# Attention tiles split into queries with keys and values, and loaded behind the score products of the step before

## The chip, the cores and the metric

One core of a Trainium2 chip runs the kernel; the seven others are idle. The metric is the device time of one execution in microseconds (us). The kernel before took 2695.2 us (median of 3 runs, 2694.12 to 2695.24).

## The reference

One layer of a hybrid decoder block on 2048 tokens of width 1024, all in float32. The change touches branch A, the attention:

```
h = RMSNorm_pre(x) * (1 + scale) + shift
q|k|v, mLSTM q|k|v|o, i|f, g_A, g_B = split(h W_in)
branch A: 8 query heads of 64 on 2 key/value heads, rotary on q and k,
          causal window of 128 in blocks of 128:
  s = q . [k of the block before | k of this block] / 8, masked
  m = max(max(s), sink);  p = exp(s - m);  p = p / (sum(p) + exp(sink - m))
  y_A = p . [v of the block before | v of this block]
branch B: conv4 + SiLU, chunkwise mLSTM, head norm, output gate -> y_B
x = x + gate * RMSNorm_post((sigmoid(g_A) y_A W_A + sigmoid(g_B) y_B W_B) W_out)
x = x + gate * RMSNorm_post(SwiGLU FFN of the normed x)
```

A block of 128 queries is one attention tile n, so there are 16 of them.

## The kernel before, in words

Every large product is written as three products of split operands (a high and a low part), so that TensorE is the engine with the most work. The first half of the program (up to about 1400 us) works on two superblocks of 1024 tokens, each of two blocks of 512 tokens. Per block it projects h with slices of `w_in`: keys and values with the gates (`tx` of 264 columns), attention queries, the mLSTM values (`vm`), and so on. The weights arrive in `raw` and are split on ScalarE and VectorE into `whi` and `wlo` (L263 to L267); the products add up in PSUM tiles `acc`, of which there are four, and ScalarE copies each out to a `tx` (L798 for keys, values and gates, L773 for queries, L819 for the mLSTM values). The rotated q, k and v of tile n are written to a DRAM buffer `at_d[n]`, by SyncE's queue (SP): 1024 columns of q (high and low part), 512 of k (high and low), 256 of v.

Attention is then a generator per stream. Stream 0 takes the even tiles and stream 1 the odd ones. One tile goes through these steps (lines of before; `attention` at L887):

- SP loads all of it, 128 x 1792, into one tile `at` (L900; the first tile of all in three pieces, L895 and L898), and the stream asks for `L_LOAD` = 5000 ns before the next step.
- TensorE makes the scores, 24 products from `at` into four PSUM tiles `mix` (L211); ScalarE copies the half that needs no mask (L923), VectorE masks the other half (L925) and takes the maximum (L930 to L933).
- ScalarE takes exp, one activation per head (L938), VectorE the sums and reciprocals (L940, L941), GpSimd normalises in two halves of four heads (L942). The stream asks for `L_SOFT` = 8000 ns.
- TensorE transposes each half (L216, `mix<-ident,tm`); ScalarE and VectorE split it (L951, L955).
- TensorE multiplies with v, which is read from the same `at` (L211, `mix<-tm,at`); L964 and L965 split the result, and SP stores it (L967).

`at` has two buffers, one per stream in effect. So the load of tile n+2 waits until the last product with v of tile n has read its `at`, and it is issued only then.

The order is decided in two stages. `run2` (L351) walks through the large products in small groups; after each group, `tick` (L230) goes on with those streams whose due time has come on a modelled clock. `finish` (L237) and `end_attention` run streams to their end with no large product between. A scheduler then puts the instructions of each engine in order. In what follows S, T and V with a number stand for the score products, the transposes and the products with v of that tile. Tiles 8 to 15 belong to superblock 1; tiles 8 to 11 run beside the projections of its second block.

Of the kernel before, what the change touches and what calls it, by code (L numbers as in the profile page):

```python
# [10 lines left out]
F32 = mybir.dt.float32  # L11
F32R = mybir.dt.float32r
# [7 lines left out]
P = 128  # L20
# [4 lines left out]
NT = TB // P  # L25
# [19 lines left out]
L_LOAD, L_HP2, L_HC = 5000.0, 1000.0, 3000.0  # L45
# [27 lines left out]
def decoder_block(ctx: ExitStack, tc: tile.TileContext, a: dict, out: bass.AP, dbg=None):  # L73
    nc = tc.nc
# [38 lines left out]
    def nm(s):  # L113
        uid[0] += 1
        return f"{s}{uid[0]}"
# [576 lines left out]
    def at():  # L692
        return kvp.tile([P, AT_N], F32R, tag="at", name=nm("at"), bufs=2)
# [34 lines left out]
    def superblock(sb):  # L728
# [158 lines left out]
        def attention(n):  # L887
            first = n == 0
# [3 lines left out]
            a_ = at()  # L892
            af = a_.bitcast(F32)
            if first:
                nc.sync.dma_start(af[:, :AT_K], at_d[n][:, :AT_K])  # L895
                for c0, k in ((AT_K, 2), (AT_V, 1)):
                    v_, d_ = (z[:, c0:c0 + 2 * k * P].rearrange("p (i u k) -> p i u k", i=k, u=2)[:, :, 1, :] for z in (af, at_d[n]))
                    nc.sync.dma_start(v_, d_)  # L898
            else:
                nc.sync.dma_start(af, at_d[n])  # L900
            qth, qtl = (a_[:, i * 512:(i + 1) * 512].rearrange("p (j q) -> p j q", j=GQ) for i in range(2))
            kth, ktl = (a_[:, AT_K + 2 * i * P:AT_K + 2 * (i + 1) * P] for i in range(2))
            vat = af[:, AT_V:].rearrange("p (u d) -> p u d", u=2)
            yield L_LOAD
# [6 lines left out]
            for jj in range(2):  # L911
# [14 lines left out]
                if jj == 0:  # L926
                    yield 0
            for g in range(2):
                hs = slice(g * GQ, (g + 1) * GQ)
                V.tensor_reduce(mx[:, hs], sc[g], axis=AX.X, op=ALU.max)  # L930
# [28 lines left out]
            for src_, u, st_, sp_ in ((pfs, int(first), True, first), (pcs, 1, False, True)):  # L959
                for g, p_ in enumerate(src_):  # L960
                    mm(yps[g * 64:(g + 1) * 64, :], vat[:, u, g * 64:(g + 1) * 64], p_.rearrange("p j q -> p (j q)"), st_, sp_)
            now[0] -= 1500.0
# [3 lines left out]
            for i, y in enumerate((yh, yl)):  # L966
                nc.sync.dma_start(y_d[b][:, i, :, t * P:(t + 1) * P], y.bitcast(F32).rearrange("p (j q) -> p j q", j=GQ))  # L967

        ready = [0]

        def attention_stream(u):
            for i in range(u, 2 * NT, 2):
                while i >= ready[0]:
                    yield 1000.0
                yield from attention(b0 * NT + i)
                done_att[0] += 1
                yield 500.0
# [1121 lines left out]
```

## Time and profile before

| what | value |
|---|---|
| median of 3 runs | 2695.2 us |
| the profiled execution | 2696.74 us |
| its span on the core | 2695.0 us |
| mean granted TensorE clock | 0.992 |
| TensorE (PE) busy | 2635.9 us, 98% |
| VectorE (DVE) busy | 1986.3 us, 74% |
| ScalarE (ACT) busy | 1297.2 us, 48% |
| GpSimd (POOL) busy | 136.8 us, 5% |
| moved by DMA | 511.89 MB, mean 190 GB/s |

The profiled execution lies 1.74 us above its span (what lies around the first and the last instruction) and 1.5 us above the median. A row of the timeline gives start, duration, engine, line, operation, `out<-in`, partitions x elements and a count of equal instructions in a row; behind it, in square brackets, stands how long the engine was idle before the row, and which instruction ended that idle time. A row of the waits gives the total, the number and the longest. In a table of windows there stands, for each engine, its busy time in that stretch, then the granted TensorE clock as a share of full speed.

### The profile page before, as it was taken

The page shows a single profiled execution, that of the slowest core. Times are in us where ns is not written, and L with a number is a line of the kernel's source. Part 1 is how long each engine was busy: PE and PEld are TensorE (multiplying, and loading weights), DVE is VectorE, ACT ScalarE, POOL GpSimd, SP SyncE. Part 2 cuts the span into 40 slices and gives each one's busy share as a digit, 9 for nine tenths or more (in the row PEclk, how much of TensorE's full clock was granted, in tenths as well). Part 3 has the DMA queues.
Part 4 walks back from the last instruction along what each step waited for, and adds up shares of the span by engine and source line. Part 5 has one row for each costly group of instructions (what it writes and reads, how often), then busy time and mean ns, then how long its engine had stood idle before and what let it go on. Part 6 is the DMA issues. An engine that isn't in the chain of part 4 may idle for free.

```text
span 2695.0 us, 35854 instructions
## 1 busy us (share of the span) xinstructions
PE 2635.9 (98%) x12382; PEld 2149.4 (80%) x12382; DVE 1986.3 (74%) x3882; ACT 1297.2 (48%) x2525; POOL 136.8 (5%) x181
## 2 busy tenths in 40 slices
PE   7899999999998999999999999999999999999998
PEld 6777788888885778888887888887877888888886
DVE  7888887768686888876687777776677676766466
ACT  4657544545754554444563443334554333333444
POOL 0100001100101000110000000000000000000000
PEclk9999999999998999999999999999999999999999
DMA  7574456897574644677775564436675232324566
GB/s 251 172 236 138 147 176 185 267 341 243 188 246 145 204 139 139 204 250 284 243 233 192 178 201 160 153 118 215 213 272 187 98 118 88 111 98 145 191 207 219
DMA packets 353637, 511.89 MB, mean 190 GB/s; under 512 B 25120, under 2 KB 213660, under 8 KB 348208
## 3 DMA queue, kind: packets, MB, share of 16 engines
q1 hardware_dynamic: 353288, 509.55, 57.2%
q8 instruction: 97, 1.59, 0.2%
q14 instruction: 84, 0.69, 0.1%
q10 hardware_dynamic: 168, 0.06, 0.0%
HBM read 357.12 MB, written 144.02 MB: 186 GB/s over the span
## 4 chain that ended last, share of the span: by engine, by line
PE 84%; DVE 6%; DMA 4%; ACT 2%; issue 1%; POOL 0%; SPq 0%; DVEq 0%; POOLq 0%; ACTq 0%
PE acc L211 59%; PE mix L211 22%; PE mix L216 2%; DVE hl L1589 1%; DMA at_d<-tx 1%; DMA raw<-as_d 1%; DMA tx<-in_w_ada_dram 1%; ACT hl L1588 1%; DMA at<-at_d 1%; DMA raw<-in_w_ffn_down_dram 1%; DVE wlo L267 0%; DMA raw<-ws_d 0%; DMA big<-big 0%; DVE tm L925 0%; DVE big L1589 0%
## 5 line engine op out<-in xcount | busy, mean ns | idle before, releaser
L211 PE MATMUL acc<-big,hl 128*128 128x512 f32 x3936 | 939.5, 393 | 2.3 <-ACT hl L1588 0.9
L211 PEld LDWEIGHTS acc<-big,hl 128*128 128x128 f32 x3936 | 732.8, 188 | 168.5 <-issue 9.0
L1588 ACT CAST hl<-raw 128x512 fp32r<-128x512 f32 x732 | 440.2, 621 | 494.9 <-PE acc L211 227.9
L1589 DVE TENSOR_TENSOR hl<-raw,hl 128x512 fp32r<-128x512 f32 x732 | 497.9, 696 | 196.5 <-ACT hl L1588 194.1
L211 PE MATMUL acc<-whi,big 128*128 128x512 f32 (+1 forms) x1216 | 356.2, 374 | 7.7 <-ACT tx L89 3.8
L211 PE MATMUL mix<-big,hl 128*128 128x512 f32 x1056 | 262.9, 390 | 1.7 <-ACT hl L1588 1.0
L211 PEld LDWEIGHTS acc<-whi,big 128*128 128x128 f32 x1216 | 222.0, 190 | 49.7 <-ACT tx L89 4.3
L211 PE MATMUL acc<-hl,hl 128*128 128x512 f32 x1008 | 237.3, 393 | 5.9 <-DVE hl L1589 3.3
L211 PEld LDWEIGHTS mix<-big,hl 128*128 128x128 f32 x1056 | 197.8, 188 | 44.4 <-ACT hl L1588 1.9
L211 PE MATMUL acc<-wlo,big 128*128 128x512 f32 (+1 forms) x608 | 225.9, 374 | 3.5 <-DVE wlo L267 3.5
L211 PEld LDWEIGHTS acc<-hl,hl 128*128 128x128 f32 x1008 | 187.0, 188 | 51.6 <-DVE hl L1589 8.7
L211 PE MATMUL mix<-hl,hl 128*128 128x512 f32 x792 | 182.3, 390 | 1.2 <-DVE ms L455 0.5
L211 PEld LDWEIGHTS mix<-hl,hl 128*128 128x128 f32 x792 | 148.0, 188 | 34.5 <-DVE hl L1589 2.9
L211 PE MATMUL acc<-big,whi 128*128 128x512 f32 x512 | 157.3, 393 | 0.0
L267 DVE TENSOR_TENSOR wlo<-raw,whi 128x1024 fp32r<-128x1024 f32 (+1 forms) x95 | 108.8, 1146 | 60.4 <-ACT whi L266 54.7
L266 ACT CAST whi<-raw 128x1024 fp32r<-128x1024 f32 (+1 forms) x95 | 93.7, 987 | 116.0 <-PE acc L211 104.7
L211 PEld LDWEIGHTS acc<-wlo,big 128*128 128x128 f32 x608 | 115.6, 190 | 24.1 <-DVE wlo L267 5.0
L457 POOL TENSOR_TENSOR rs<-ms,halves 128x1 f32<-128x1 f32 (+1 forms) x56 | 42.9, 779 | 1657.0 <-DVE ms L455 1647.2
L211 PE MATMUL mix<-hcT4h,hl 128*128 128x512 f32 x352 | 115.6, 389 | 0.7 <-ACT hl L1588 0.7
L211 PE MATMUL acc<-hcT2h,hl 128*128 128x512 f32 x352 | 115.5, 389 | 0.0
L211 PEld LDWEIGHTS acc<-big,whi 128*128 128x128 f32 x512 | 95.3, 188 | 19.2
L211 PE MATMUL acc<-big,wlo 128*128 128x512 f32 x256 | 97.5, 392 | 0.0
(350 smaller groups left out, 3544.2 us busy)
## 6 DMA issues: line engine op xcount, KB each, us to landing
raw<-in_w_in_dram SPq DMA_DIRECT2D x48, 1024.0 KB, 5.6
as_d<-w SPq DMA_DIRECT2D x154, 256.0 KB, 2.0
raw<-as_d SPq DMA_DIRECT2D x70, 512.0 KB, 3.9
raw<-in_w_ffn_gate_dram SPq DMA_DIRECT2D x22, 1024.0 KB, 5.7
raw<-in_w_ffn_up_dram SPq DMA_DIRECT2D x22, 1024.0 KB, 5.5
raw<-ws_d SPq DMA_DIRECT2D x40, 512.0 KB, 4.6
y_d<-tm SPq DMA_DIRECT2D x64, 256.0 KB, 3.7
tx<-in_w_ada_dram SPq DMA_DIRECT2D x64, 256.0 KB, 4.2
```

Source lines behind the costliest of these rows:

```text
L211: T.matmul(o, lhsT=lhsT, rhs=rhs, start=start, stop=stop, skip_group_check=resumed)
L216: T.transpose(o, i, ident[:k, :k])
L266: A.copy(hv, src)
L267: V.tensor_tensor(lv, src, hv.bitcast(F32), op=ALU.subtract)
L457: G.tensor_tensor(r[:, :n], ms[:, :n], nhalf[:, :n], op=ALU.pow)
L1588: A.copy(v(hi), src)
L1589: V.tensor_tensor(v(lo), src, v(hi).bitcast(F32), op=ALU.subtract)
```

## The change

`at` is split into two tiles: `at` (q and k, 128 x 1536) and `av` (v, 128 x 256), with two buffers each and the same space in all. The score products read `at`, the products with v read `av`; so the buffer of q and k comes free with the scores of its tile. Where the stream's next tile n+2 lies in a block that is ready (n = 0, 1, 4, 5 within a superblock of eight tiles), `load_qk(n + 2)` is issued right behind the score products of n, and `load_v(n + 2)` behind its products with v; the stream then goes to the next tile without `L_LOAD`. These loaded-ahead tiles are n = 2, 3, 6, 7 and 10, 11, 14, 15. The eight others (0, 1, 4, 5, 8, 9, 12, 13) are loaded when the stream begins or finds its block ready, in two DMAs instead of one, with `L_LOAD` behind them. Nothing else is edited; lines behind L889 move by up to 23 (scores' copy L936, exp L953, normalising L957, keys' copy L801, queries' copy L776, mLSTM values' copy L822). Every engine has the same instructions in both programs, but SP, which issues 15 DMAs more.

```diff
--- before.py
+++ after.py
@@ -689,8 +689,11 @@
 
     AT_K, AT_V, AT_N = 2 * 512, 2 * 512 + 4 * P, 2 * 512 + 6 * P
 
-    def at():
-        return kvp.tile([P, AT_N], F32R, tag="at", name=nm("at"), bufs=2)
+    def at_qk():
+        return kvp.tile([P, AT_V], F32R, tag="at", name=nm("at"), bufs=2)
+
+    def at_v():
+        return kvp.tile([P, AT_N - AT_V], F32, tag="av", name=nm("av"), bufs=2)
 
     def ld(shape, dtype=F32):
         t = kvp.tile([P, 512], dtype, tag="ld", name=nm("ld"), bufs=4)
@@ -884,24 +887,34 @@
             R["gates", b] = negm_d, mp, cl, ex
 
 
-        def attention(n):
+        def load_qk(n):
+            a_ = at_qk()
+            af = a_.bitcast(F32)
+            if n == 0:
+                nc.sync.dma_start(af[:, :AT_K], at_d[n][:, :AT_K])
+                v_, d_ = (z[:, AT_K:AT_V].rearrange("p (i u k) -> p i u k", i=2, u=2)[:, :, 1, :] for z in (af, at_d[n]))
+                nc.sync.dma_start(v_, d_)
+            else:
+                nc.sync.dma_start(af, at_d[n][:, :AT_V])
+            return a_
+
+        def load_v(n):
+            v_ = at_v()
+            if n == 0:
+                nc.sync.dma_start(v_[:, P:], at_d[n][:, AT_V + P:])
+            else:
+                nc.sync.dma_start(v_, at_d[n][:, AT_V:])
+            return v_
+
+        def attention(n, a_, av, ahead):
             first = n == 0
             b, t = divmod(n, NT)
             k0 = P if first else 0
             ks = slice(k0, 2 * P)
-            a_ = at()
-            af = a_.bitcast(F32)
-            if first:
-                nc.sync.dma_start(af[:, :AT_K], at_d[n][:, :AT_K])
-                for c0, k in ((AT_K, 2), (AT_V, 1)):
-                    v_, d_ = (z[:, c0:c0 + 2 * k * P].rearrange("p (i u k) -> p i u k", i=k, u=2)[:, :, 1, :] for z in (af, at_d[n]))
-                    nc.sync.dma_start(v_, d_)
-            else:
-                nc.sync.dma_start(af, at_d[n])
+            later = None
             qth, qtl = (a_[:, i * 512:(i + 1) * 512].rearrange("p (j q) -> p j q", j=GQ) for i in range(2))
             kth, ktl = (a_[:, AT_K + 2 * i * P:AT_K + 2 * (i + 1) * P] for i in range(2))
-            vat = af[:, AT_V:].rearrange("p (u d) -> p u d", u=2)
-            yield L_LOAD
+            vat = av.rearrange("p (u d) -> p u d", u=2)
             mx = small.tile([P, HQ], F32, tag="mx", name=nm("mx"))
             nm_ = small.tile([P, HQ], F32, tag="nmx", name=nm("nmx"))
             sums = small.tile([P, HQ], F32, tag="sums", name=nm("sums"))
@@ -925,6 +938,8 @@
                     V.copy_predicated(dst, mk, negc.unsqueeze(1).to_broadcast([P, 2, P]) if first else bv[:, :, :P])
                 if jj == 0:
                     yield 0
+            if ahead():
+                later = load_qk(n + 2)
             for g in range(2):
                 hs = slice(g * GQ, (g + 1) * GQ)
                 V.tensor_reduce(mx[:, hs], sc[g], axis=AX.X, op=ALU.max)
@@ -959,20 +974,28 @@
             for src_, u, st_, sp_ in ((pfs, int(first), True, first), (pcs, 1, False, True)):
                 for g, p_ in enumerate(src_):
                     mm(yps[g * 64:(g + 1) * 64, :], vat[:, u, g * 64:(g + 1) * 64], p_.rearrange("p j q -> p (j q)"), st_, sp_)
+            if later is not None:
+                later = later, load_v(n + 2)
             now[0] -= 1500.0
             yh, yl = tm([P, 512], F32R), tm([P, 512], F32R)
             A.copy(yh, yps)
             V.tensor_tensor(yl, yps, yh.bitcast(F32), op=ALU.subtract)
             for i, y in enumerate((yh, yl)):
                 nc.sync.dma_start(y_d[b][:, i, :, t * P:(t + 1) * P], y.bitcast(F32).rearrange("p (j q) -> p j q", j=GQ))
+            return later
 
         ready = [0]
 
         def attention_stream(u):
+            tiles = None
             for i in range(u, 2 * NT, 2):
-                while i >= ready[0]:
-                    yield 1000.0
-                yield from attention(b0 * NT + i)
+                n = b0 * NT + i
+                if tiles is None:
+                    while i >= ready[0]:
+                        yield 1000.0
+                    tiles = load_qk(n), load_v(n)
+                    yield L_LOAD
+                tiles = yield from attention(n, *tiles, lambda: i + 2 < ready[0])
                 done_att[0] += 1
                 yield 500.0
 
```

On TensorE the two programs differ in two stretches, one in each superblock (in time about 95 to 290 us and 775 to 990 us); all that stands between and behind them has the same order. Three places follow.

**TensorE, tiles 10 and 11.** In these rows `at_7797` is tile 10 and `at_7831` tile 11, `tm_7840` and `tm_7841` are the two halves of the probabilities of tile 10, `tm_7918` and `tm_7919` those of tile 11. Before, from the last score product of tile 11 to the first of its products with v:

```order
L211 MATMUL mix_7939<-at_7831 128x256
L216 MATMUL mix_7997<-ident,tm_7840 128x128 x4
L216 MATMUL mix_8027<-ident,tm_7841 128x128 x4
L211 MATMUL mix_8042<-tm_8002,at_7797 64x512
L211 MATMUL mix_8042<-tm_8032,at_7797 64x512
L211 MATMUL mix_8042<-tm_8004,at_7797 64x512
L211 MATMUL mix_8042<-tm_8034,at_7797 64x512
L216 MATMUL mix_8053<-ident,tm_7918 128x128 x4
L216 MATMUL mix_8071<-ident,tm_7919 128x128 x4
L211 MATMUL mix_8089<-tm_8058,at_7831 64x512
```

After, the rows from the last scores of tile 11 on; `at_7724` is its q and k, `tm_7826` and `tm_7827` belong to tile 10, and `acc_8288` is one of the four tiles of the query projection:

```order
L211 MATMUL acc_8288<-whi_8379,big_7150 128x512
L211 MATMUL mix_7937<-at_7724 128x256 x6
L216 MATMUL mix_7980<-ident,tm_7826 128x128 x4
L216 MATMUL mix_7999<-ident,tm_7827 128x128 x4
L211 MATMUL acc_8288<-wlo_8380,big_7150 128x512
L211 MATMUL acc_8288<-whi_8379,big_7151 128x512
```

Before, S10, S11, T10, V10, T11 and V11 stood in one block, with no large product between them from S10 to the first `acc` behind V11. After, products of the query projection and of `vm` stand between nearly all of them (17 between T10 and V10, 6 between V10 and T11), and the loads of q and k of tiles 10 and 11 stand on SP behind S8 and S9.

**ScalarE, between the keys and the queries of superblock 1's second block.** `acc_8016` to `acc_8019` are the four PSUM tiles of the key and value projection, `tm_7587` and `tm_7588` the scores of tile 8. Before:

```order
L263 CAST whi_8170<-raw_7745 128x2x4x64 x2
L798 COPY tx_8182<-acc_8016 128x264
L881 ACT_TABLE_LOAD
L881 ACTIVATE ex_7654<-ex_7654 128x48
L798 COPY tx_8204<-acc_8017 128x264
L798 COPY tx_8224<-acc_8018 128x264
L263 CAST whi_8257<-raw_7745 128x2x4x64 x2
L798 COPY tx_8244<-acc_8019 128x264
L938 ACTIVATE tm_7587,sums_7585<-tm_7587,nmx_7584 128x128
L934 ACTIVATE es_7586<-es_7586 128x8
L938 ACTIVATE tm_7587,sums_7585<-tm_7587,nmx_7584 128x128 x3
L938 ACTIVATE tm_7588,sums_7585<-tm_7588,nmx_7584 128x128 x4
```

After, where the four are `acc_8088` to `acc_8091`, the scores of tile 8 are `tm_7606` and `tm_7607`, and those of tile 9 begin with `tm_7686`:

```order
L263 CAST whi_8186<-raw_7768 128x2x4x64 x2
L953 ACTIVATE tm_7606,sums_7604<-tm_7606,nmx_7603 128x128
L949 ACTIVATE es_7605<-es_7605 128x8
L953 ACTIVATE tm_7606,sums_7604<-tm_7606,nmx_7603 128x128 x3
L953 ACTIVATE tm_7607,sums_7604<-tm_7607,nmx_7603 128x128 x4
L801 COPY tx_8200<-acc_8088 128x264
L263 CAST whi_8278<-raw_7768 128x2x4x64 x2
L953 ACTIVATE tm_7686,sums_7684<-tm_7686,nmx_7683 128x128
L949 ACTIVATE es_7685<-es_7685 128x8
L953 ACTIVATE tm_7686,sums_7684<-tm_7686,nmx_7683 128x128 x3
L953 ACTIVATE tm_7687,sums_7684<-tm_7687,nmx_7683 128x128 x4
L801 COPY tx_8223<-acc_8089 128x264
```

The exps of tile 8 moved ahead of the first copy out of `acc`, and those of tile 9 ahead of the second.

**TensorE, the first scores of tile 12.** `at_8655` and `at_8681` are its q and k, `acc_8464` to `acc_8467` and `acc_8487` to `acc_8490` the products of `vm`, `tx_8459` and `tx_8473` rotated queries. Before, the end of `vm` and the first two score rows:

```order
L211 MATMUL acc_8467<-wlo_8560,big_7135 128x512
L211 MATMUL acc_8467<-whi_8559,big_7136 128x512
L211 MATMUL acc_8467<-whi_8559,big_7135 128x512
L211 MATMUL acc_8467<-wlo_8560,big_7135 128x512
L211 MATMUL acc_8467<-whi_8559,big_7136 128x512
L211 MATMUL mix_8755<-at_8655 128x256
L211 MATMUL mix_8756<-at_8655 128x256
```

After:

```order
L211 MATMUL acc_8489<-whi_8554,big_7150 128x512
L211 MATMUL acc_8490<-whi_8554,big_7150 128x512
L216 MATMUL mix_8530<-ident,tx_8459 128x128 x4
L216 MATMUL mix_8539<-ident,tx_8473 128x128 x4
L216 MATMUL mix_8722<-ident,gt 36x128 x4
L211 MATMUL mix_8782<-at_8681 128x256 x6
L211 MATMUL acc_8487<-wlo_8555,big_7150 128x512
L211 MATMUL acc_8487<-whi_8554,big_7151 128x512
```

The first six score products of tile 12 moved ahead of the last 44 products of `vm`; the other way round, only 28 such products stand between the transposes of the first rotated queries (whose result is stored to `at_d[12]`) and the scores that read it back, where there were 66.

## The prediction

> **What bounds the kernel now.** I read the page first, then TensorE's waits, then windows of the two stretches in which its order changes, then the timeline of those windows.
>
> ```profile
> PE 2635.9 (98%) x12382; PEld 2149.4 (80%) x12382; DVE 1986.3 (74%) x3882; ACT 1297.2 (48%) x2525; POOL 136.8 (5%) x181
> ```
> TensorE is the bound: 98% busy, 59 us idle in 2695. No product is added or removed, so this change can win only idle time and time at a low clock, and only in the two stretches that it reorders.
>
> ```profile
> PE mix L216 <- POOL tm L942: 8.4, 6, 3.4
> PE mix L211 <- DMA at<-at_d: 4.1, 3, 3.4
> ```
> The wait that the change is about, scores for their load, costs 4.1 us in all, 3.4 of it in one place. More would have to come from what that place does to its surroundings.
>
> ```profile
> 770.00:805.00 35.00, 31.78 (x205) 27.88 (x204) 29.43 (x90) 19.51 (x52) 0.00 (x0) 0.95 0.75 253
> 840.00:875.00 35.00, 30.40 (x144) 20.80 (x145) 23.43 (x60) 18.88 (x58) 4.68 (x5) 0.81 0.44 126
> 875.00:910.00 35.00, 34.30 (x184) 27.46 (x183) 32.05 (x68) 20.08 (x42) 0.00 (x0) 1.00 0.76 271
> ```
> The stretch 840 to 875 is the worst: 4.6 us without a busy TensorE, and the granted clock at 0.81 where the next stretch has 1.00.
>
> ```profile
> 833.07 0.97 PE L211 MATMUL mix<-at 64*128 64x256 f32 x12
> 833.97 1.07 PE L211 MATMUL mix<-tm,at 128*64 128x512 f32 x2
> ...
> 836.51 0.97 PE L211 MATMUL mix<-at 64*128 64x256 f32 x6 [0.57 <-DVE tm L965]
> 840.86 2.93 PE L211 MATMUL mix<-at 64*128 64x256 f32 x24 [3.37 <-DMA at<-at_d]
> 845.22 1.97 PE L216 MATMUL mix<-ident,tm 128*128 128x128 f32 x8 [1.43 <-DVE tm L925]
> ...
> 852.22 0.66 PE L216 MATMUL mix<-ident,tm 128*128 128x128 f32 x4 [1.42 <-POOL tm L942]
> 853.77 1.12 PE L216 MATMUL mix<-ident,tm 128*128 128x128 f32 x4 [0.90 <-POOL tm L942]
> 854.81 1.97 PE L211 MATMUL mix<-tm,at 128*64 128x512 f32 x2
> ```
> These are tiles 10 and 11 in one block without large products: S10's end, S11 behind its load, T10, T11, V11. The idle time is 0.57 + 3.37 + 1.43 + 1.42 + 0.90 = 7.7 us.
>
> **What goes.** *S11's load.* It is issued behind V9:
>
> ```profile
> 835.07 0.33 SPq L900 DMA_DIRECT2D at<-at_d  x1
> ```
> The change issues q and k behind S9 (in time about 794), 40 us ahead, and the order now puts products of the query projection and of `vm` between these steps. So 3.37 and 0.57 go. T10 now stands about 12 us behind S10's end (37 products at about 0.23, tile 11's 24 scores, four products with v and T9's second half), and needs GpSimd's second half:
>
> ```profile
> 843.43 1.04 POOL L942 TENSOR_TENSOR tm<-tm,sums 128x512 f32<-128x512 f32 x1 [29.33 <-DVE sums L941]
> 844.97 1.04 POOL L942 TENSOR_TENSOR tm<-tm,sums 128x512 f32<-128x512 f32 x1 [0.50 <-ACT tm L923]
> ```
> S10 ended at 836.51 + 0.97 = 837.5, so the halves were ready 7.0 and 8.5 us later with little else in the queues. 1.43 goes too: 5.4 us in all. T11 keeps its waits: it stands 7.0 us behind S11, against the same 7.0 and 8.5; I leave 1.42 + 0.90 as they are.
>
> *The low clock.* 24 scores took 2.93 where 12 take 0.97 (1.0 too many), eight transposes 1.97 where four take 0.66 (0.65), four 1.12 (0.46), two products with v 1.97 for 1.07 (0.90): 3.0 us, which I let go with the idle time that came before it.
>
> *The copy behind the casts.*
>
> ```profile
> 781.11 2.18 ACT L535 CAST big<-big 128x512 fp32r<-128x512 f32 x4 [2.23 <-DMA big<-big]
> 784.10 0.39 PE L211 MATMUL acc<-whi,big 128*128 128x264 f32 x1 [2.93 <-ACT tx L819]
> 787.61 1.67 PE L211 MATMUL mix<-at 64*128 64x256 f32 x12
> ```
> TensorE waited for a copy out of `acc` that stood behind four casts; in the new ScalarE order it stands behind two. Half of 2.18 goes: 1.1 us.
>
> *T12.*
>
> ```profile
> 904.67 6.96 PE L211 MATMUL acc<-big,hl 128*128 128x512 f32 x30
> 913.07 0.66 PE L216 MATMUL mix<-ident,tm 128*128 128x128 f32 x4 [1.43 <-POOL tm L942]
> ...
> 914.76 1.11 PE L216 MATMUL mix<-ident,tm 128*128 128x128 f32 x4
> 915.53 3.76 PE L211 MATMUL acc<-big,hl 128*128 128x512 f32 x10
> ```
> Idle 1.43, and behind it ten products in 3.76 where 30 take 6.96 (1.4 too many) and a transpose group 0.45 too long: 3.3 us. T12 moves from 8.4 to 11.3 us behind S13. Between 0 and 3.3, I take 3.0. Sum of what goes: 5.4 + 3.0 + 1.1 + 3.0 = **12.5 us**.
>
> **What comes.** *The start of the query projection.*
>
> ```profile
> 796.14 1.14 ACT L263 CAST whi<-raw 128x512 fp32r<-128x512 f32 x2 [2.11 <-PE acc L211]
> 797.39 0.38 ACT L798 COPY tx<-acc 128x264 f32<-128x264 f32 x1
> 797.79 1.28 ACT L881 ACT_TABLE_LOAD   x1
> ...
> 801.08 0.42 ACT L938 ACTIVATE tm<-tm,nmx 128x128 f32<-128x128 f32 x1
> ...
> 803.89 0.40 ACT L938 ACTIVATE tm<-tm,nmx 128x128 f32<-128x128 f32 x1
> ```
> Eight exps take 801.08 to 804.3, 3.2 us. All four copies out of the key and value projection stood ahead of them; now the first stands behind tile 8's exps, the second behind tile 9's. From S9's end ScalarE has two copies (0.8 with the handover), the table load 1.3, a small exp 0.2, two casts 1.0, the exps 3.2, the copy 0.4: 6.9 us, where TensorE is through with 47 small products of 0.12 after 5.7. Wait 1.2. The second copy comes 1.1 + 3.2 + 0.4 = 4.7 later, TensorE 12 products and T8 later (3.6): wait 1.1. Together **2.3**; between 0 (tile 8's maximum comes late, and the program's order does not bind) and 4.
>
> *S12 behind its load.*
>
> ```profile
> 864.26 0.60 PE L216 MATMUL mix<-ident,tx 128*128 128x128 f32 x4
> 864.62 0.48 PE L211 MATMUL acc<-whi,big 128*128 128x512 f32 x1
> ...
> 881.65 0.98 PE L211 MATMUL mix<-at 64*128 64x256 f32 x12
> ```
> ```profile
> 870.11 0.38 SPq L900 DMA_DIRECT2D at<-at_d  x1
> ```
> ```profile
> DMA to landing us min/median/max: 5.8/6.2/10.0
> ```
> Tile 12 is not loaded ahead: its load waits for the rotated queries, whose transposes end at 864.6. It is issued 5.5 us later and lands 5.8 or more after that, in time for S12 at 881.65. Now S12 follows after 28 products (0.23 each by the 30 in 6.96) and four groups of transposes (864.62 - 864.26 = 0.36 each): 7.8 us. With 1536 of 1792 columns I estimate the landing between 5.0 (by size) and 5.8, and take 5.4: 5.5 + 5.4 - 7.8 = **3.1 us** of new wait. The ends are 2.7 and, with the longest landing of 10.0, 7.7.
>
> *Superblock 0.*
>
> ```profile
> 128.47 0.66 PE L216 MATMUL mix<-ident,tm 128*128 128x128 f32 x4 [0.35 <-POOL tm L942]
> 131.90 0.94 PE L211 MATMUL mix<-at 64*128 64x256 f32 x6 [0.17 <-DMA at<-at_d]
> 139.41 0.97 PE L211 MATMUL mix<-at 64*128 64x256 f32 x6
> 146.09 1.70 PE L211 MATMUL mix<-at 64*128 64x256 f32 x24 [0.60 <-DMA at<-at_d]
> 155.42 2.82 POOL L942 TENSOR_TENSOR tm<-tm,sums 128x512 f32<-128x512 f32 x2 [27.00 <-DVE sums L941]
> 160.79 1.04 POOL L942 TENSOR_TENSOR tm<-tm,sums 128x512 f32<-128x512 f32 x1 [2.54 <-DVE sums L941]
> ```
> Both load waits and 0.35 go (1.1 us). But T2 now stands 9.6 us behind S2, where tile 2's probabilities took from 140.4 to 156.5 at the earliest, 16.1 us, and tile 3's 14.0. These long times were in rows where nobody waited; tile 10's 7.0 is the other end. New waits at T2 and T3 lie between 0 and 6.5; by the new VectorE order, which takes tile 2's maxima early, I take 2.5. Net +1.4, between -1.1 and +5.4.
>
> The 15 extra DMAs cost 0.33 us of SP's time each, by the row of 835.07, and no engine waits for SP there: the loads of v have until the transposes. I count 0.
>
> **Sum.** -12.5 + 2.3 + 3.1 + 1.4 = -5.7 us on the profiled execution's 2696.7, so 2691.0 by its own time; it lies 1.5 above the median, so **2689.5**, 0.21% faster.
>
> [...]
>
> **Rivals.**
> *Slower: the probabilities come late.* The new order gives each tile a shorter way from scores to transposes: about 13 us for tile 8, 12 for 9 and 10, 7 for 11, 9.6 for 2. If a tile in this busy stretch takes not 7 to 8.5 us but 14, as tile 3 did, T8 waits 1 more, T10 2, T11 4.7 beyond what I left it, T2 about 2: some 10 us, 2699.5. At 16.1 it is 19 us, 2708. Break-even with before is at about 13 us. For it: tiles 2 and 3, and VectorE busy 29.4 of 35 us in 770 to 805. Against: the exps were put early in the new order. I take 2703.
> *No change: the wait moves to S12.* If its load, with 2 MB of others issued behind it, takes the longest landing, it is 4.6 us more, and a gap of 7.7 costs low clock as the gap of 3.37 did (3.0): 2697. Against: half of its landings took 6.2 or less.
> *Faster: the copies out of `acc` wait for nobody* and T2 is in time: 2.3 and 2.5 less, 2684.7.
> That the loads are not ahead at all is excluded for tiles 10 and 11 by SP's order.
>
> **How the numbers follow.** The forecast gets 0.45, between 2685.5 and 2693.5; no change at S12 0.22; faster 0.16; slower 0.17. About 0.2% (5.4 us) is what a measurement of this kernel can tell from no change, so the limits are 2689.8 and 2700.6. Of the forecast 0.25 lie below 2689.8: faster 0.41; slower 0.15 (the rest of its case is under 2700.6); same 0.44. The range leaves out the lower end of the faster case and the slower one's bulk: 2683.5 to 2701.
>
> **What would show it.** Right: no wait of S11 for a DMA, PEclk near 1.00 where V10 and V11 now are, S12 with a DMA wait of about 3 us, the first query products waiting about 1 us for L801. Wrong: POOL L957 as the releaser of 3 us and more before T2, T8, T10 or T11; S12 waiting over 6; a half-speed stretch elsewhere.

## The result, and the profile after

| what | before | after |
|---|---|---|
| median of 11 runs each | 2694.7 us | 2701.8 us |
| the profiled execution | 2696.74 us | 2701.84 us |
| its span | 2695.0 us | 2700.1 us |
| TensorE busy | 2635.9 us | 2641.6 us |

The change makes the kernel slower: the ratio is 1.0022, with a 95% interval from 1.0012 to 1.0033. That is 7 us more, where 5.7 us less was forecast. The profile of before lies above its median and the profile of after does not, so the two traces differ by 5.1 us and not by 7.

The first line of the page has the answer to where the time went:

```profile
PE 2641.6 (98%) x12382; PEld 2149.8 (80%) x12382; DVE 1986.3 (74%) x3882; ACT 1298.6 (48%) x2525; POOL 139.1 (5%) x181
```

TensorE has the same 12382 products and is busy 5.7 us longer, which is more than the whole 5.1 us. Its idle time went from 59.1 to 58.5 us, so the waits that went and the waits that came balance. These are TensorE's waits of after:

```profile
PE mix L216 <- POOL tm L957: 4.6, 4, 3.2
PE mix L211 <- DMA at<-at_d: 3.6, 2, 3.1
PE acc L211 <- ACT tx L801: 3.3, 1, 3.3
PE acc L211 <- ACT tx L822: 2.2, 2, 1.5
```

Transposes wait 3.8 us less for GpSimd; the wait for a load has moved from S11 to S12 and is nearly as long; and 3.3 us of waiting for a copy out of `acc` (L801) are new.

The costliest groups say which products got longer. A row has the busy time of a group, the mean of one product, then the idle time ahead of it. First before, then after:

```profile
L211 PE MATMUL acc<-whi,big 128*128 128x512 f32 (+1 forms) x1216 | 356.2, 374 | 7.7 <-ACT tx L89 3.8 <-ACT tx L819 2.9 <-ACT tx L798 0.9
L211 PE MATMUL acc<-wlo,big 128*128 128x512 f32 (+1 forms) x608 | 225.9, 374 | 3.5 <-DVE wlo L267 3.5
L216 PE MATMUL mix<-ident,tm 128*128 128x128 f32 (+1 forms) x272 | 45.7, 287 | 9.9 <-POOL tm L942 8.4 <-DVE tm L925 1.4
L211 PE MATMUL mix<-at 64*128 64x256 f32 (+1 forms) x384 | 40.8, 302 | 4.7 <-DMA at<-at_d 4.1 <-DVE tm L965 0.6
```

```profile
L211 PE MATMUL acc<-whi,big 128*128 128x512 f32 (+1 forms) x1216 | 359.3, 376 | 9.9 <-ACT tx L89 3.8 <-ACT tx L801 3.3 <-ACT tx L822 2.2
L211 PE MATMUL acc<-wlo,big 128*128 128x512 f32 (+1 forms) x608 | 228.8, 378 | 3.3 <-DVE wlo L267 3.3
L216 PE MATMUL mix<-ident,tm 128*128 128x128 f32 (+1 forms) x272 | 42.7, 278 | 5.8 <-POOL tm L957 4.6 <-DVE tm L938 1.2
L211 PE MATMUL mix<-at 64*128 64x256 f32 (+1 forms) x384 | 45.4, 301 | 3.7 <-DMA at<-at_d 3.6
```

The same 384 score products cover 45.4 us instead of 40.8, and the projections' products 3.1 and 2.9 us more; of these groups only the transposes cover less, by 3.0. The mean of one score product is the same (302 and 301 ns). So they did not get slower: fewer of them ran beside another one, as the counts below show (in superblock 0 54 instead of 62, in superblock 1 52 instead of 66). The products with v, as a group, changed little over the whole program (48.8 us before, 48.5 after):

```profile
L211 PE MATMUL mix<-tm,at 128*64 128x512 f32 x124 | 48.8, 643 | 0.0
L211 PE MATMUL mix<-tm,av 128*64 128x512 f32 x124 | 48.5, 615 | 0.0
```

Where in the program this happens is seen by the time between the same two places in TensorE's order. From the 443rd to the 1440th product (about 97 to 297 us of before, attention of superblock 0) before needs 198.95 us and after 206.19, **7.2 us more**. From the 3000th to the 4900th (about 615 to 1019 us, superblock 1) it needs 403.56 and 400.90, **2.7 us less**. The start is 1.8 us shorter, about what superblock 0 is idle longer (1.6); the remaining 2.4 of the 5.1 us lie in stretches that the change does not touch.

One place of superblock 0 shows the mechanism. TensorE's timeline of after, at V1 and S3:

```profile
125.88 0.98 PE L211 MATMUL mix<-at 64*128 64x256 f32 x12
...
131.47 1.07 PE L211 MATMUL mix<-tm,av 128*64 128x512 f32 x2
132.47 0.50 PE L211 MATMUL mix<-at 64*128 64x256 f32 x2
132.90 1.08 PE L211 MATMUL mix<-tm,av 128*64 128x512 f32 x4
133.91 0.73 PE L211 MATMUL mix<-at 64*128 64x256 f32 x4
134.57 0.51 PE L211 MATMUL acc<-whi,big 128*128 128x264 f32 x2
135.01 1.07 PE L211 MATMUL mix<-tm,av 128*64 128x512 f32 x2
136.01 0.97 PE L211 MATMUL mix<-at 64*128 64x256 f32 x6
136.91 0.39 PE L211 MATMUL acc<-wlo,big 128*128 128x264 f32 x1
137.14 0.41 PE L211 MATMUL acc<-whi,big 128*128 128x264 f32 x2
137.48 0.97 PE L211 MATMUL mix<-at 64*128 64x256 f32 x6
```

Read the rows in pairs. One product with v shows as two records (x2) in this trace and takes 1.07 us; two that follow each other and write to different halves of the columns (x4) take 1.08 together: they run side by side. Twelve score products that alternate between the two halves of the rows take 0.98, and six of one half take 0.97. Here S3 has lost its order: a few scores, a product with v, a few scores, products of the projection, and then six of one half and six of the other. A product that stands alone takes the time of two in these rows. And where the form changes, between products on half of the rows, on half of the columns and on the whole array, time is added: two of the projection's products start at 134.57 and the next thing at 135.01, 0.44 us, where two in a longer row need 0.24 (from 129.36 to 130.09 seven start 0.12 us apart). That is about 0.2 us more; what TensorE does in it, the trace does not show.

Counted over the 443rd to the 1440th product, in us, where a record counts as beside another if the next one of its kind starts less than 0.06 us later:

| kernel | idle | scores (records beside another) | products with v (records beside another) | large products (rows of them) | transposes |
|---|---|---|---|---|---|
| before | 5.4 | 18.9 (62) | 20.7 (18 of 60) | 138.6 (42) | 15.4 |
| after | 7.1 | 20.5 (54) | 23.0 (14 of 60) | 140.6 (52) | 15.1 |

The sum is 5.6 us more of work and 1.6 us more of idle time. Prices fitted to these rows, an estimate: 0.107 us for a score that lost its neighbour, 0.43 for such a record of a product with v, 0.14 (products with v) to 0.2 for a change of form. The row of six scores bears them out: from 136.01 to the next start at 136.91 it is 0.90, and six times 0.107 and one change make 0.84. Eight scores and three more changes make 1.5 of the measured 1.6; four records with v and four changes 2.3 of 2.3; ten more rows of large products 2.0 of 2.0. As the prices were fitted to these three sums, that they come out proves nothing; e1 and e9 below are the test. The last one is coarse as well, for transposes break rows of large products too, and these changes are free: outside the low clock, four transposes in a row have 0.11 us from start to start and a large product of 512 columns has 0.23; the last transpose ahead of a large product has 0.03, and that product 0.31. Next to scores or products with v a large product has 0.32 (ahead of them) or 0.34 (behind them). There are 13 more of these in after, about 1.3 us, and 0.4 us only moved over from the transposes.

Superblock 1 got what the prediction promised and lost it again. Three windows of after, whose stretches were shown of before (all stands about 5 us later here, the 3700th product at 761.8 for 756.6, so that a window holds nearly but not quite the same work):

```profile
770.00:805.00 35.00, 30.21 (x197) 26.00 (x197) 28.06 (x73) 17.62 (x42) 0.00 (x0) 0.95 0.91 311
840.00:875.00 35.00, 30.35 (x149) 21.62 (x148) 26.52 (x60) 15.45 (x39) 2.60 (x3) 0.97 0.60 195
875.00:910.00 35.00, 35.00 (x169) 27.39 (x169) 28.38 (x67) 20.41 (x53) 1.61 (x2) 0.94 0.73 261
```

The granted clock of 0.81 in the second is gone (0.97), but the third now has 0.94 where it had 1.00, and in the first TensorE is busy 1.6 us less (30.21 for 31.78). From the 3700th to the 4900th product idle time fell by 2.8 us, transposes by 2.1 and products with v by 2.8; scores rose by 2.3 (52 beside another instead of 66) and large products by 2.7. The waits behind this, from TensorE's timeline:

```profile
784.36 0.39 PE L211 MATMUL acc<-whi,big 128*128 128x264 f32 x1 [0.69 <-ACT tx L822]
788.69 0.39 PE L211 MATMUL acc<-whi,big 128*128 128x264 f32 x1 [1.52 <-ACT tx L822]
790.26 0.64 PE L211 MATMUL acc<-whi,big 128*128 128x264 f32 x3 [0.57 <-ACT whi L266]
807.26 0.50 PE L211 MATMUL acc<-whi,big 128*128 128x512 f32 x1 [3.29 <-ACT tx L801]
852.19 0.66 PE L216 MATMUL mix<-ident,tm 128*128 128x128 f32 x4 [0.53 <-POOL tm L957]
868.76 0.66 PE L216 MATMUL mix<-ident,tx 128*128 128x128 f32 x4 [1.00 <-DVE tx L756]
872.98 1.61 PE L211 MATMUL mix<-at 64*128 64x256 f32 x6 [3.12 <-DMA at<-at_d]
```

The wait of 3.29 at the start of the query projection is longer than the copies of the prediction explain. Followed back, it is a chain of three engines. ScalarE's timeline, VectorE's, and SP's, all of after, and then SP's row and VectorE's of before:

```profile
802.48 0.24 ACT L884 ACTIVATE ex<-ex 128x48 f32<-128x48 f32 x1 [2.41 <-DVE ex L883]
```

```profile
802.16 0.18 DVE L881 SCALAR_TENSOR_TENSOR ex<-cl,mp 128x16 f32<-128x16 f32 x1 [2.00 <-DMA mp<-sm_d]
```

```profile
798.48 0.34 SPq L870 DMA_DIRECT2D mp<-sm_d  x1
```

```profile
793.29 0.33 SPq L867 DMA_DIRECT2D mp<-sm_d  x1
```

```profile
796.09 0.18 DVE L878 SCALAR_TENSOR_TENSOR ex<-cl,mp 128x16 f32<-128x16 f32 x1 [0.29 <-DMA mp<-sm_d]
```

VectorE waits 2.0 us for a small load of the gates (`mp`), ScalarE's small exp 2.4 us for VectorE, and behind that exp stand tile 8's exps and the copy L801 for which TensorE waits. The load is issued 5.2 us later by the clock than before, but so is all else here, so it is not late by itself. What moved is the exp: before, two casts and a copy out of `acc` stood ahead of it on ScalarE, and now they stand behind it. Its table load starts at 798.79 where it started at 797.79, 4.2 us earlier when measured against the rest. From its issue to VectorE's use the load took 3.7 us where it took 2.8; whether the early loads of q and k did that was not tried by itself.

### The profile page after: what moved, and what is told of

It is laid out like the page before. It is cut to its first block, busy times and chain, and to the rows that moved or that the text cites. A ratio compares the mean times of both kernels' runs of the same rounds, so it can differ in the third digit from the quotient of the medians.

```text
span 2700.1 us, 35893 instructions
## 1 busy us (share of the span) xinstructions
PE 2641.6 (98%) x12382; PEld 2149.8 (80%) x12382; DVE 1986.3 (74%) x3882; ACT 1298.6 (48%) x2525; POOL 139.1 (5%) x181
## 4 chain that ended last, share of the span: by engine, by line
PE 84%; DVE 5%; DMA 4%; ACT 2%; issue 1%; SPq 0%; POOL 0%; DVEq 0%; POOLq 0%; ACTq 0%
PE acc L211 59%; PE mix L211 24%; PE mix L216 2%; DVE hl L1612 1%; DMA big<-big 1%; DMA raw<-as_d 1%; ACT hl L1611 1%; ACT tm L953 0%; DMA raw<-ws_d 0%; DMA mp<-sm_d 0%; DVE wlo L267 0%; DMA at<-at_d 0%; DMA tx<-in_w_ada_dram 0%; DMA at_d<-tx 0%; DMA sm_d<-sm 0%
## 5 line engine op out<-in xcount | busy, mean ns | idle before, releaser
L267 DVE TENSOR_TENSOR wlo<-raw,whi 128x1024 fp32r<-128x1024 f32 (+1 forms) x95 | 108.9, 1146 | 65.5 <-ACT whi L266 61.2
```

The lines of the kernel that those rows point to most:

```text
L267: V.tensor_tensor(lv, src, hv.bitcast(F32), op=ALU.subtract)
```

## The experiments

Two theories. **A**: TensorE pays for mixing. The steps of two tiles now become ready together, their small products get interleaved with each other and with the projections, pairs are lost and forms change more often. **B**: TensorE pays for waiting. With `L_LOAD` gone, steps follow too soon, and each waits for an exp, a copy or a load. Numbers in brackets behind a ratio are the 95% interval. The times of stretches are those of one profile each, and superblock 1 can differ by some 5 us between two profiles of one order (e1, e2 and e4, below), so there the medians carry the verdict.

**Which part costs.** Four kernels ran beside before (2693.98 us). *e1_split_only* splits the tile, and no stream asks for a load ahead:

```diff
-                tiles = yield from attention(n, *tiles, lambda: i + 2 < ready[0])
+                tiles = yield from attention(n, *tiles, lambda: False)
```

> Only the split of the attention tile, nothing loaded ahead: every tile is loaded when its stream comes to it, with the 5000 ns behind it. Theory A (TensorE pays for mixing: a score product or a product with v runs beside its partner of the other half only when the two stand next to each other, and each change of form costs about 0.2 us): the new order has 44 instead of 56 paired score products in superblock 0 and 45 instead of 63 in superblock 1, at 0.107 us each 3.2 us, and about nine more changes of form, 1.8 us; so 3 to 5 us slower than before, with the load waits still there. Theory B (the loss comes from attention steps that follow too soon, waits for exps, copies and GpSimd): with the old spacing nothing is lost, within 1.5 us of before.

Measured: 2694.79 us, 1.0005 [0.9995, 1.0015]. As a time this is B's answer, and not A's 3 to 5 us. In the trace, scores and large products of superblock 0 cost 3.1 us more, as A said (53 scores beside another instead of 62), but transposes and idle time give 2.1 back. By the prices fitted above, 9 scores, 4 rows of scores and 5 of large products make 2.8 of these 3.1. The split by itself costs nothing that can be measured.

The edit leaves out less than it was meant to. SP's row for q and k of tile 11 in e1:

```profile
798.62 0.34 SPq L898 DMA_DIRECT2D at<-at_d  x1
```

That is right behind S9, as in after (798.91), and not behind V9 as in before (835.07). With v in a tile of its own the buffer is free, and the scheduler moves the load up without being asked. So e1 has the early loads too, and its expectation that the load waits stay did not hold: no score product between 95 and 1000 us waits for a load.

*e2_ahead_with_wait* asks for the loads ahead, and keeps the 5000 ns:

```diff
                     tiles = load_qk(n), load_v(n)
-                    yield L_LOAD
+                yield L_LOAD
```

> q, k and v are loaded ahead as in the change, but a stream still asks for the 5000 ns before each tile, so the steps keep the spacing of e1 and TensorE's order has the same counts as e1. Theory A: e1's cost of 3 to 5 us of mixing stays; the wait of 3.4 us for the load of tile 11 and the low clock behind it (3 us) go: 1 to 4 us faster than before, 5 to 7 faster than e1. Theory B: nothing of the mixing, so 6 to 7 us faster than before.

Measured: 2695.14 us, 1.0002 [0.9993, 1.0012], neither A's 1 to 4 us nor B's 6 to 7. In the traces every engine of e2 has the instructions of e1 in the order of e1, so the two are one program measured twice: the split, early loads, and the 5000 ns kept. Superblock 1's stretch is 1.1 us shorter than before in one profile and 4.2 in the other, which no edit explains. The wait of S11 for its load is gone in both, and a wait for GpSimd stands a little behind it, at T10 (here of e2):

```profile
843.88 1.11 PE L216 MATMUL mix<-ident,tm 128*128 128x128 f32 x4 [5.23 <-POOL tm L957]
```

TensorE's idle time from the 3000th to the 4900th product is 16.1 us before, 16.4 in e1 and 16.1 in e2: the wait moved on. So early loads alone show neither a cost nor a gain; the cost comes with the missing 5000 ns, in which after differs from these two.

*e3_ahead_sb1* and *e4_ahead_sb0* ask for the loads ahead, and so go without the 5000 ns, in one superblock each:

```diff
-                tiles = yield from attention(n, *tiles, lambda: i + 2 < ready[0])
+                tiles = yield from attention(n, *tiles, lambda: b0 > 0 and i + 2 < ready[0])
```

```diff
-                tiles = yield from attention(n, *tiles, lambda: i + 2 < ready[0])
+                tiles = yield from attention(n, *tiles, lambda: b0 == 0 and i + 2 < ready[0])
```

> The change in superblock 1 only; superblock 0 as in e1. Theory A: superblock 0 loses about 3 us of mixing, superblock 1 gains the 2.4 us that the trace of the change shows there: within 2 us of before. Theory B: superblock 0 loses nothing, so 2 to 3 us faster than before.

> The change in superblock 0 only; superblock 1 as in e1. Theory A: superblock 0 loses its 7 us (5.6 of them in busy time of TensorE by the trace of the change), superblock 1 about 1 to 2 us of mixing: 7 to 9 us slower than before. Theory B: superblock 0 loses what it waits more there, 1.6 us, and superblock 1 nothing: 1 to 2 us slower.

Measured: 2694.51 us for superblock 1 alone, 1.0000 [0.9991, 1.0009]; 2698.6 us for superblock 0 alone, 1.0015 [1.0002, 1.0028]. The first is within A's 2 us and shows nothing of B's 2 to 3; its order in superblock 1 is not quite after's (61 scores and 14 records of products with v beside another, after 52 and 18). The loss is superblock 0's. In e4's trace the stretch is 7.6 us longer, after's 7.2 again, with TensorE's order there that of after (54 scores and 14 products with v beside another, 52 rows of large products). The median shows 4.6 us of it, which lies below A's 7 to 9 and above B's 1 to 2. And e1 and e4 run one order in superblock 1, yet their profiles differ there by 4.8 us against before (-1.1 and -5.9), with another granted clock over the whole profiled run (0.992 in e1's, 0.994 in e4's).

**How much room the steps need.** Four kernels beside before (2695.14 us). *e6_ahead_1500* and *e7_ahead_3500* put a shorter wait in the place of none; *e8_mixed_spacing* puts 5000 ns in superblock 0 and 1500 in superblock 1. For e6 (e7 has 3500.0):

```diff
                     yield L_LOAD
+                else:
+                    yield 1500.0
```

and for e8:

```diff
                     yield L_LOAD
+                elif b0 > 0:
+                    yield 1500.0
+                else:
+                    yield L_LOAD
```

> As e2, with 1500 ns instead of 5000 before a tile that was loaded ahead (the change has none). Theory A, by the counts of its order (48 paired score products, 9 runs of paired products with v, 21 + 20 + 52 changes of form in superblock 0; 51, 10, 18 + 20 + 41 in superblock 1): superblock 0 at +1 to +3 us against before, far from the +7.2 of the change; superblock 1 at -3 to -5, since 2 us of the change's mixing are gone. Theory B: with the spacing cut by 70%, superblock 0 should be at +5 and more.

> As e2, with 3500 ns. Theory A, by the counts (44 paired score products, 8 runs of paired products with v, 23 + 21 + 52 changes of form in superblock 0: 1.6 us more mixing than e2): superblock 0 at +2 to +4 us, more than e6 although the steps are further apart; superblock 1 as e2, -3 to -5. Theory B: superblock 0 between e2 (+1.1) and e6.

> A try for a better version: loads ahead in both superblocks, the old 5000 ns before a tile in superblock 0 and 1500 in superblock 1. Both theories: superblock 0 at about +1 as in e2. Superblock 1 -3 to -5 us by theory A. In all 2 to 4 us faster than before, hardly to be told from no change.

Measured: 2698.57 us, 1.0011 [0.9999, 1.0022]; 2698.99 us, 1.0018 [1.0007, 1.0030]; and 2690.51 us, 0.9986 [0.9975, 0.9997]. The first two can't be told apart. In superblock 0 e6's stretch is 7.0 us longer than before, which is B's 5 and more and not A's 1 to 3; but it starts 3.7 us earlier, and its profile is one of 2694.6 us, 4 below its median, which does not show the loss. e7's is 3.9 longer, which fits both. What is more in e6 is idle time (8.5 us, with 56 scores beside another), in e7 form (53 scores, 16 records of products with v, idle 5.0): nothing follows for A or B. e8 is 4.6 us faster than before by the medians, a little more than the 2 to 4 that both expected. It has the order of e1 in superblock 0, where as many records of products with v stand beside another as in before (18; 21.3 us for after's 23.0). In superblock 1 no score waits for its load, as in e1 and e2, which gain nothing; TensorE is idle 13.5 us there where these have 16.1 and more. Which of this makes the 4.6 us was not tried by itself.

*e5_before_unpaired* was to price the pairs by taking them away in before, with the loop over the two halves outside:

```diff
-                    for lt, rt, st_, sp_ in ((qth, kth, True, False), (qth, ktl, False, False), (qtl, kth, False, True)):
-                        for g in range(2):
+                    for g in range(2):
+                        for lt, rt, st_, sp_ in ((qth, kth, True, False), (qth, ktl, False, False), (qtl, kth, False, True)):
```

> The kernel before with one thing changed: the three score products of one half of the heads are written before those of the other half, instead of in turn, so that fewer of them stand next to their partner. Its order has 39 instead of 56 paired score products in superblock 0 and 37 instead of 63 in superblock 1. Theory A: at 0.107 us a lost pair 4.6 us more busy time of TensorE, 1.8 in superblock 0 and 2.8 in superblock 1, a little of it given back or added by other changes of the order: 3 to 6 us slower than before. Theory B (waits only): nothing, within 1.5 us.

Measured: 2695.0 us, 0.9997 [0.9985, 1.0009]. Its premise fell: 66 scores of superblock 0 still ran beside another, four more than in before. Three products of one half next to three of the other pair up as well, by this count. The run says nothing on the price.

**The disputed cost by itself.** If A is right, products with v that stand together must win where they are mixed. In the program a tile's four products come in the order: block before with head group 0, with 1, this block with 0, with 1. The first can start when half of the transposes is through, so others slip in between. Reversed, the first product needs what is ready last, and the four go in one piece. It is the same sum with its terms in another order. Three kernels beside before (2694.61 us): after with this edit (*e9_change_v_together*), before with it (*e10_before_v_together*), e8 with it (*e11_mixed_v_together*):

```diff
-            for src_, u, st_, sp_ in ((pfs, int(first), True, first), (pcs, 1, False, True)):
-                for g, p_ in enumerate(src_):
+            for src_, u, st_, sp_ in ((pcs, 1, True, False), (pfs, int(first), first, True)):
+                for g, p_ in reversed(list(enumerate(src_))):
```

> The change, with the four products with v of a tile written in the opposite order: first the two from the half that ScalarE and VectorE finish last, then the other two. They add to the same sums, so TensorE can no longer start the first of them early and must make all four in a row. In its order they stand in 8 runs per superblock instead of 22 and 20, and the big products are taken up again 36 and 32 times instead of 53 and 41. Theory A, with 0.43 us for a product that finds its partner, 0.2 for a change of form: 16 to 20 us less busy time of TensorE than the change in the two superblocks, and 8 to 13 us faster than before if the waits stay as they are. Theory B: the products with v come later, nothing else: as slow as the change or slower, 4 to 8 us slower than before.

> The same edit on the kernel before: 8 runs of products with v per superblock instead of 18 and 21. Theory A: 8 to 12 us faster than before. Theory B: within 1.5 us of before, or slower.

> The same edit on e8 (loads ahead, 5000 ns before a tile in superblock 0 and 1500 in superblock 1). Theory A: e8's gain of 4 us and another 8 to 11: 10 to 15 us faster than before, the best of the three. Theory B: as e8, 2 to 5 us faster.

Measured: **2682.96 us** for the change with this edit, 0.9960 [0.9948, 0.9973]; 2692.11 us for before with it, 0.9991 [0.9982, 1.0000]; 2684.78 us for e8 with it, 0.9968 [0.9951, 0.9985]. e9 is 11.7 us faster than before, as A says and against B, and 18.8 us faster than after's median. e11 is 9.8 us faster, just short of A's 10 to 15 and far from B's 2 to 5; it is not the best of the three, and can't be told from e9. e9's group of products with v and one piece of its timeline:

```profile
L211 PE MATMUL mix<-tm,av 128*64 128x512 f32 x124 | 32.1, 639 | 3.7 <-DVE tm L970 3.7
```

```profile
134.80 1.94 PE L211 MATMUL mix<-tm,av 128*64 128x512 f32 x8
```

Four products with v (x8) take 1.94 us, two pairs, where after's rows at 131.47, 132.90 and 135.01 take 1.07, 1.08 and 1.07 for the same four. Over the program they cover 32.1 us, and in after 48.5. The mean of one is much the same (639 and 615 ns). By the prices fitted above, 30 more records beside another and 26 rows less make 16.5 of these 16.4 us, so here the prices hold where they were not fitted. The scores give 3.1 us more (45.4 to 42.3).

This prices the mixing; it does not undo the change's own loss. The products with v cover as much before as after (48.8 and 48.5): they lost 2.3 us in superblock 0 and won 2.8 in superblock 1, and e9 takes away a cost that before has too. For the scores and the large products, the rest of the loss, A rests on the counts.

e10 is where A alone fails: it is 2.5 us faster, where A says 8 to 12 and B at most 1.5. The first line of its page, and TensorE's waits of 95 to 1000 us; then those of e9 in the same stretch:

```profile
PE 2621.4 (97%) x12382; PEld 2148.6 (80%) x12382; DVE 1989.3 (74%) x3882; ACT 1299.1 (48%) x2525; POOL 141.7 (5%) x181
```

```profile
PE mix L216 <- POOL tm L942: 7.9, 6, 2.8
PE mix L211 <- DMA at<-at_d: 3.9, 3, 2.3
PE mix L211 <- DVE tm L955: 3.4, 4, 1.4
PE acc L211 <- ACT tx L773: 3.3, 3, 1.1
PE acc L211 <- DVE wlo L267: 3.0, 3, 1.6
PE mix L216 <- DVE tm L925: 3.0, 1, 3.0
PE acc L211 <- ACT tx L819: 2.9, 1, 2.9
PE acc L211 <- ACT tx L798: 2.5, 2, 2.2
```

```profile
PE mix L216 <- POOL tm L957: 5.3, 3, 3.9
PE mix L211 <- DVE tm L970: 3.7, 3, 2.1
...
PE mix L211 <- DMA at<-at_d: 0.8, 2, 0.6
```

TensorE is busy 14.5 us less than in before (2621.4 for 2635.9), which is A's price or more, and its span is only 4.6 us shorter: 9.9 us came back as idle time. Loads and GpSimd are not what came back: these waits are as long as in before (8.4 and 4.1). New are the products with v waiting for the last split of the probabilities (L955, 3.4) and the copies of the queries (L773, 3.3); those of keys and values (L798, 2.2 more), the mask (L925, 1.6 more) and the weights' split (L267, 1.1 more) are longer. I read it so that the lone products had been the cover under which this work of ScalarE and VectorE came in time; for L955 the new order itself is a cause, since the first product now needs what is ready last. In e9 TensorE is busy 2620.6 us in a span of 2681.1, so 8.5 us less is idle than in e10, 3.1 of them in the wait for loads and 2.6 in that for GpSimd. e9 and e10 differ by the change alone, and by 9.1 us in their medians: **the change is worth that much once the products with v stand together**, and costs 7 where they don't.

So the loss follows A as far as the counts and the fitted prices go, and waits as in B decide how much of a gain is left; neither alone gives all eleven times. What is not settled: the 1.6 us of idle time within superblock 0's 7.2, the difference between e4's trace and its median, and why e6 and e7 take what they take. That the scores stay together as well was not tried.

## Why the prediction was wrong, point by point

*What bounds.* TensorE is the bound: right. "This change can win only idle time and time at a low clock": this sentence failed. It took the busy time of the same products as given, and that is what moved, by 5.7 us.

*S11's load, 5.4.* Right: no wait of S11 for a DMA is left, nor the waits ahead of it and behind it.

*T11.* Left at 1.42 + 0.90; measured 0.53. 1.8 us better than the sum has it.

*The low clock, 3.0.* Right at its place: the window there went from 0.81 to 0.97. But the sum had no low clock behind the new waits, and there is one behind both long ones: six scores at 872.98, behind S12's wait, take 1.61 where six take 0.97, and the window of 875 to 910 fell from 1.00 to 0.94; behind the wait of 3.29 that of 805 to 840 fell from 1.00 to 0.95. In after the granted clock is 0.50 from 873 to 879 and from 808 to 811. A half-speed stretch elsewhere was one of the prediction's own signs of being wrong.

*The copy behind the casts, 1.1.* Wrong: 2.93 became 0.69 + 1.52 + 0.57 = 2.8. A shorter queue ahead of the copy split the wait, it did not end it.

*T12, 3.0.* Right: it waits no more.

*The start of the query projection, 2.3.* The first wait was put at 1.2 and took 3.29; the second did not come. Mis-sized by 1.0, and for another reason: I followed ScalarE's own work and not what VectorE and SP bring it. It was within its bound of 4.

*S12, 3.1.* Right to the tenth, 3.12, and the tenth is luck. The landing was right: 5.5 us from the issue at 867.47, put at 5.4. But the load was issued 7.2 us behind the transposes that end at 860.2, not 5.5, and TensorE took 9.6 us from there to S12's place, not 7.8, with a wait of 1.0 for L756 in between. The errors of 1.7 and 1.8 took each other away.

*Superblock 0, 1.4.* **This is the step that failed.** T2 and T3 do not wait, so the 2.5 put there was too much. But the stretch is 7.2 us longer, 5.5 net of the earlier start, and 5.6 of the 7.2 are products that stand alone or change form. This was in no term. My own quoted rows showed it: twelve scores in 0.97 at 833.07 and six in 0.97 at 836.51, in one fence. I read the second as a wait's row and did not ask why half as many take as long.

*The sum for superblock 1*, 12.5 - 2.3 - 3.1 = 7.1 less, was 2.7 less in the trace, and nothing in e3's median. Its idle part came out: the sum's own terms of idle time (5.4 + 1.1 + 1.4 of T12 - 2.3 - 3.1) make 2.5 less, measured 2.8. That is partly luck too: T11 came out 1.8 better, the copy and the query projection 1.0 worse each. Its part of low clock (3.0 + 1.6 of T12) makes 4.6; transposes and products with v fell by 4.9. What took it back, 2.3 us of scores and 2.7 of large products, has the cause that superblock 0 has, as far as the scores go; of the large products two more rows explain 0.4, and the clock of 0.94 would explain about 2 (0.06 of 35 us), which was not tried by itself.

*The rivals.* "The probabilities come late" had the right sign and by luck nearly the right time (2703); its mechanism is not what happened: transposes wait less for L957, not more (in e1 and e2 T10 does wait 5.2 for it, without a loss). "The wait moves to S12" had the place and the low clock behind it right, and 3.1 of its 7.7 us came. None of the rivals had the mechanism that decided.

## What to carry to other kernels

TensorE's busy time was no constant here: the same 12382 products took 2635.9 us before, 2641.6 after and 2621.4 in e10. So before a reordering of small products that run in pairs is priced, count the neighbours, and look in the trace for rows where half as many products take as long (here six scores in 0.97 us, as twelve). Steps that became ready together got mixed here (52 rows of large products in superblock 0 instead of 42), so whoever frees a step from a wait should also say what keeps its products in one piece; here the order of four products did, and it turned 7 us of loss into 12 us of gain. And measures are not to be judged one by one: the change alone lost 7 us, the products with v in one piece alone won 2.5, and both together won 11.7. And look in the trace whether an edit left out what it was to leave out: splitting the tile was enough for the loads to come early.

## What the runs showed of the hardware

- Two products with v on different halves of the columns take 1.08 us, one takes 1.07 (after, at 132.90 and 131.47); two pairs in a row take 1.94 (e9, at 134.80).
- Twelve scores on alternating halves of the rows take 0.98 us, six of one half 0.97 (after, at 125.88 and 136.01). With three of one half written ahead of three of the other, 66 scores of superblock 0 ran beside another (e5), with the halves in turn 62 (before): strict alternation in the program was not needed.
- Two of the projection's products take 0.44 us between other forms (after, at 134.57) and 0.24 in a row: about 0.2 us for the change, an estimate from these rows. Between transposes and products of the projection, both on the whole array, none shows (0.03 + 0.31 us from start to start at the change, 0.11 + 0.23 in a row).
- With TensorE's order the same in a stretch of 400 us, two profiles differed by 4.8 us there (e1 and e4); with the order the same on every engine, by 3.1 (e1 and e2).
